# Two bursts of small matmuls joined, the last head's pauses, the prompt state in halves, and longer rows

## The chip, the cores and the metric

The kernel runs on one core of a Trainium2 chip. The metric is the time of one execution on the device in microseconds (us); the time given for a kernel is the median of its runs. Engines: PE does the matmuls (PEld is its weight load), DVE is the vector engine, ACT the scalar engine, POOL the general one, SP issues most of the DMAs.

## The reference

One step of a decoder layer for a prompt of 256 positions and eight samples of 8 positions each, 320 columns in all, at a width of 2048:

```python
u = x @ w_in
q, k, v, o_pre, i_pre, f_pre, z, xbc, dt_pre = split_columns(u, SPLIT_SIZES)
h_m, C, n, m = mlstm_mixer(...)      # 4 heads of 256; states C (256 x 256), n, m
h_s, S, sconv = ssd_mixer(...)       # 16 heads of 64, 2 groups
mix = concatenate([h_m, h_s]) @ w_out
x = layer_norm(ALPHA * x + mix, ln1_g, ln1_b)
f, fconv = conv_ffn(x, w_up, f_conv_w, f_conv_b, w_down, fconv0)
x = layer_norm(ALPHA * x + f, ln2_g, ln2_b)
```

For the mLSTM heads, with `w_inter`, `w_end` and `decay` from the gates:

```python
num = einsum('btsh,bshe->bthe', s, v) + w_inter[..., None] * einsum('bthd,bhde->bthe', q, C)
C_new = decay[..., None, None] * C + einsum('bsh,bshd,bshe->bhde', w_end, k, v)
```

The samples start from given states (for the mLSTM 8 x 4 matrices of 256 x 256); the prompt starts from zero, and its final state `p_C`, `p_n` is returned as well. All is in float32.

## The kernel before, in words

**The main stream.** The four projections (in, out, up, down) are a stream of matmuls with 128 x 128 weights. Each weight tile is split into a high part (ACT, line 74) and a remainder (DVE, line 75), the activations too (XH/XL, MH/ML, HH/HL, and DH/DL, which the trace calls `big`), and each product is three matmuls: hi x high, hi x low, lo x high. `run_groups` walks over groups of two units (128 output columns each; four units in the first group of a projection) in slices of four 128-deep steps, so twelve matmuls. Splits are issued four slices ahead of their use. Two PSUM banks of eight are held by a group of two.

**The tasks.** All other work (gates, SSD, mLSTM, norms) is written as generators. After each slice `tasks.pump(1300)` lets those that are due take steps: at most six steps, and none more once 1300 ns of planned PE time are used. A clock `tasks.clk` counts planned nanoseconds: 0.424 a column for a matmul of the main stream, so 1628 for a slice, and 1.69 a column for a plain float32 matmul. `yield 500` makes a task due 500 planned ns later, but it resumes only after a slice; a `yield` without a number means 2500. The order in which the Python code issues instructions is the order on every engine and on each DMA queue: an engine that reaches an instruction which must wait holds back all behind it. A PSUM bank can be given out again once its last reader has been issued; the matmul that takes it then waits until that reader is done.

**mLSTM samples** (`ml_chunks`, from line 1156): for each head h and each half x of the samples, the products of q with four states (8 calls with 32 output rows each, 128 x 32 weights) go to one bank, ACT scales them (L1200), POOL's queue sends the wanted rows to `VT` (`gather`, L813). After `yield 500` the updates follow: 8 matmuls with 32 x 128 weights from `kv` into four banks, then DVE (L1212) makes decay x state + update. After `yield 1500` SP stores the states (L1179) and loads those needed two rounds later (L1172); then `yield 5000`.

**Scores and heads.** `ml_scores` for a head h > 1 waits for flag `("pv", h-2)`, has SP fetch a broadcast row (`Mb` from `d_m`, L1067), yields 4000, and then issues DVE, ACT and PE work on it (L1074, L1076, L1081, L1082). `ml_out(h)` waits for `("acc", h)`, set when the last chunk of head h is done, yields 2500, multiplies the scores with `VT` (128 x 258 matmuls), sets `("pv", h)`, and normalizes the head: statistics on DVE, `rsqrt` in three rounds with a pause after each, then scale and bias by ACT (L1261), a last pause, and transposes (L238, with ACT copying out at L1269). Then `o_task` multiplies by the gate (L1284) and `mix_parts` splits the result (L1314, L1315) and sets `("mix", 3)`. The first group of the out projection calls `ensure(("mix", s))` ahead of each slice s.

**The end.** After the down projection the second norm's mean and scale are formed (L1671 to L1675), transposed on PE, copied by DVE to `nbr` (L1682), and for each of four column blocks c three matmuls with `rows` give the bias `w`; ACT scales (L1699) and copies `w` (L1701), POOL adds (L1702), ACT's queue sends `y_sample` (L1704, L1709); for the prompt DVE does it in one operation (L1707) and SP sends it. In between stands `p_state`: the prompt's mLSTM state, for each head two units (e = 0, 1) of matmuls over 258 columns into one bank, a copy by ACT (L1607), a DMA by SP (L1608) and a copy of one column to `pn` by POOL (L193). `pn` is transposed on PE in block 2, copied by ACT (L1692) and sent by POOL (L1693).

**The rows.** `big` tiles (DH, DL, dd) have 16 rows of NX = 322 columns: the first part of the up projection runs on 322 columns, as two more carry the first norm's gain and bias; parts 2 and 3 use 320 of them. XH, MH and HH have rows of 320.

Of the kernel before, what the change touches and what calls it, by code (L numbers as in the profile page):

```python
# [7 lines left out]
F32R = mybir.dt.float32r  # L8
# [5 lines left out]
NT = 320  # L14
# [156 lines left out]
def _hybrid_step(ctx, tc, I, O):  # L171
# [638 lines left out]
    def gather(out, y):  # L810

        for c in range(4):
            gdma(out[8 * c:8 * c + 8], y[32 * c:32 * c + 8])  # L813
# [342 lines left out]
    def ml_chunks():  # L1156

        yield from wait("setup")
        c_src, c_dst = I["state_mlstm_C"][0], O["s_C"][0]
        wb = box["wb"]  # L1160
        n0v = n0f.rearrange("p (b h e) -> p b h e", h=4, e=2)
        cts = {}

        def dram(t, n):
            h, x = divmod(n, 4)
            return [t[2 * x + b, h].rearrange("(e p) f -> p e f", p=128) for b in range(2)]

        def load(n):
            h, x = divmod(n, 4)
            t = mt("T4", [128, 2, 2, 258])  # L1170
            for b, d in enumerate(dram(c_src, n)):
                dma(t[:, b, :, 0:256], d)  # L1172
            pcopy(t[:, :, :, 256:257], n0v[:, 2 * x:2 * x + 2, h, :].unsqueeze(3))
            cts[n] = t

        def store(n):
            t = cts.pop(n)
            for b, d in enumerate(dram(c_dst, n)):
                dma(d, t[:, b, :, 0:256])  # L1179

        for n in range(4):
            load(n)
        yield 2000
        for h in range(4):
            yield from wait(("q", 2 * h + 1))
            qz = box["qz"][h % 2]
            pcopy(qz[:, :, :, 0:8], box["Q"][:, 2 * h:2 * h + 2, 256:NT].rearrange("p e (b t) -> p e b t", t=8))
            flags.add(("qz", h))
            yield from wait(("kv", h))
            kv = box.pop(("kv", h))  # L1190
            yield 5000
            for x in range(2):
                n0 = 4 * h + 2 * x
                ps = bank()
                for e in range(2):
                    for b in range(4):
                        mm(ps[32 * b:32 * b + 32, 0:257], qz[:, e, 4 * x + b, :], cts[n0 + b // 2][:, b % 2, e, 0:257],
                           e == 0, e == 1)
                yi = mt("T2", [128, 258])
                A.activation(yi[:, 0:257], ps[:, 0:257], AF.Copy, scale=TT3[:, x, 96 + h:97 + h])  # L1200
                gather(box["VT"][32 * x:32 * x + 32, 2, h, 0:257], yi[:, 0:257])
                yield 500
                pss = [bank() for _ in range(4)]
                for e in range(2):
                    for b in range(4):
                        r = slice(32 * b, 32 * b + 32)
                        mm(pss[b][:, 256 * e:256 * e + 256], kv[r, 0, x, 128 * e:128 * e + 128], kv[r, 1, x, :], True, True)
                tasks.clk -= 6 * 108
                for b in range(4):
                    bb = 4 * x + b  # L1210
                    cb = cts[n0 + b // 2][:, b % 2, :, 0:256]
                    V.scalar_tensor_tensor(cb, cb, wb[:, h, 64 + bb:65 + bb], pss[b].rearrange("p (e f) -> p e f", e=2),  # L1212
                                           ALU.mult, ALU.add)
                yield 1500
                for n in (n0, n0 + 1):
                    store(n)
                for n in (n0 + 4, n0 + 5):
                    if n < 16:
                        load(n)
                yield 5000 if n0 < 14 else 0  # L1220
            flags.add(("acc", h))

    def ml_out(h):
        if h:
            yield from wait(("pv", h - 1))
        yield from wait(("P", h), *[("v", 2 * h + e) for e in range(2)])
        yield 3000
        VT, P, Q = box["VT"], box.pop(("P", h)), box["Q"]
        num = mt("T4", [128, 3, 258])
        ps = bank()  # L1230
        mm(ps[:, 0:258], P[:, 0:128], VT[:, 0, h, :], True, True)
        A.activation(num[:, 0, :], ps[:, 0:258], AF.Copy)
        yield 0
        ps = bank()
        mm(ps[:, 0:258], P[:, 128:256], VT[:, 0, h, :], True, False)
        mm(ps[:, 0:258], P[:, 256:384], VT[:, 1, h, :], False, True)
        A.activation(num[:, 1, :], ps[:, 0:258], AF.Copy)
        yield 0
        yield from wait(("acc", h))
        yield  # L1240
        ps = bank()
        mm(ps[:, 0:258], P[:, 384:512], VT[:, 2, h, :], True, True)
        A.activation(num[:, 2, :], ps[:, 0:258], AF.Copy)
        flags.add(("pv", h))
        yield
        st6, mv = sm([128, 3, 6]), sm([128, 3, 2])
        for i in range(3):
            V.bn_stats(st6[:, i, :], num[:, i, 0:256])
            V.bn_aggr(mv[:, i, :], st6[:, i, :])
        den, sc, nbias, var = (sm([128, 3]) for _ in range(4))  # L1250
        V.scalar_tensor_tensor(den, num[:, :, 256], -1.0, num[:, :, 256], ALU.mult, ALU.max)
        V.tensor_tensor(den, den, TT1[:, :, 64 + h], ALU.max)
        V.reciprocal(den, den)
        V.tensor_tensor(var, den, den, ALU.mult)
        V.tensor_tensor(var, var, mv[:, :, 1], ALU.mult)
        rs = yield from rsqrt(mp, var, GN_EPS, [128, 3], 1500 if h < 3 else 0)
        V.tensor_tensor(sc, den, rs, ALU.mult)
        V.scalar_tensor_tensor(nbias, mv[:, :, 0], -1.0, sc, ALU.mult, ALU.mult)
        yield
        for i in range(3):  # L1260
            A.activation(num[:, i, 0:256], num[:, i, 0:256], AF.Identity, scale=sc[:, i:i + 1],  # L1261
                         bias=nbias[:, i:i + 1])
        yield from wait(("qz", h))
        yield 8000 if h < 3 else 3000
        for e in range(2):
            ps = bank()
            for i in (2, 0, 1):
                transpose(ps[:, TS[i]], num[:, i, 128 * e:128 * e + 128])
            A.activation(Q[:, 2 * h + e, :], ps[:, 0:NT], AF.Copy, scale=col(C_NM + 2 * h + e))  # L1269
            yield 0  # L1270
        flags.add(("hn", h))
# [73 lines left out]


    fp = ctx.enter_context(tc.tile_pool(name="fp", bufs=1))
    NX = NT + 2
    fr = tile_of(fp, {"big": (3, 16 * NX), "c": (12, 346), "rx": (2, 4 * NT), "rows": (2, 2304), "dg": (2, 384)})

    def fsm(shape, dt=F32):
        return fp.tile(shape, dt, name=nm("fsm"))
# [33 lines left out]
        rx[c] = t  # L1386

    load_rx(0)
    dd = fr("big", [128, 16, NX])
    DH, DL = fr("big", [128, 16, NX], F32R), fr("big", [128, 16, NX], F32R)  # L1390
    s1, s2, kbc = fr("c", [128, NT]), fr("c", [128, NT]), fr("c", [128, NT])

    def out_task(m, ps):
# [191 lines left out]
    def p_operands():  # L1585

        yield from wait(("h", 42), "gb")
        yield 10000
        fin["k"], fin["v"] = [], {}
        for i in range(2):  # L1590
            t = fr("rx", [128, 4, 256])
            dma(t, d_kt[:, i, :, :])
            fin["k"].append(t)
            yield 5000
        for h in range(4):
            for i in range(2):
                fin["v"][i, h] = fr("c", [128, 258])
                dma(fin["v"][i, h], d_vt[:, i, h, :])
            yield 5000

    def p_state(h):
        for e in range(2):
            ps = bank()
            for i in range(2):
                mm(ps[:, 0:258], fin["k"][i][:, h, 128 * e:128 * e + 128], fin["v"][i, h], i == 0, i == 1)
            t = fr("c", [128, 258])
            A.activation(t, ps[:, 0:258], AF.Copy)  # L1607
            dma(O["p_C"][0, 0, h, 128 * e:128 * e + 128, :], t[:, 0:256])  # L1608
            pcopy(pn[:, 2 * h + e:2 * h + e + 1], t[:, 256:257])

    def gb_rows():

# [60 lines left out]
    V.scalar_tensor_tensor(nb2, mv[:, :, 0], -1.0, rs, ALU.mult, ALU.mult)  # L1673
    V.tensor_copy(nbc[:, :, 0:2], bcl(nb2, 2))
    V.tensor_tensor(nbc[:, :, 2], nb2, f32(nbc[:, :, 0]), ALU.subtract)  # L1675
    for h in range(3):
        p_state(h)
    ps = bank()
    for i in range(3):
        transpose(ps[0:5, 128 * i:128 * i + 128], f32(nbc[:, i, :]))  # L1680
    times_g(15, fin["pt"])
    V.tensor_copy(nbr, ps[0:5, 0:384])  # L1682
    ys = O["y_sample"].rearrange("b t f -> (b t) f")
    for c in range(4):
        s = slice(512 * c, 512 * c + 512)
        if c == 1:
            p_state(3)
        if c == 2:
            pt = bank()
            transpose(pt[0:8, 0:128], pn)  # L1690
            po = fsm([8, 128])
            A.activation(po, pt[0:8, 0:128], AF.Copy)  # L1692
            gdma(O["p_n"][0, 0].rearrange("h (e p) -> (h e) p", p=128), po)  # L1693
# [80 lines left out]
```

## Time and profile before

| | us |
|---|---|
| median of 3 runs | 1540.66 (1540.61, 1540.66, 1542.48) |
| the profiled execution: its own time | 1537.98 |
| its span | 1536.2 |
| PE busy in it | 1515.6 (99%) |
| DVE / ACT / POOL busy | 979.2 / 773.3 / 313.5 |

A timeline row has start, duration, engine, line, operation, tiles and shapes, a count where like ones are merged, and in brackets the idle time of the engine before it and what ended it. A matmul's duration there contains its latency: the distance of two starts is what a matmul takes from the stream. A row of groups ends with busy time, mean ns of one, and idle time before. A row of the chain has start, duration and what was at work.

### The profile page before, as it was taken

To read this page: it belongs to the slowest core of one execution; us is meant where nothing else is said; L and a number is where in the kernel's file an instruction comes from. 1 tells how busy PE (TensorE), PEld (TensorE's weight loads), DVE (VectorE), ACT (ScalarE), POOL (GpSimd) and SP (SyncE) were. 2 spreads that over 40 slices of the span, in tenths; PEclk is the share of its full clock that TensorE was granted. 3 is DMA by queue.
4 is the path that set the end of the run, shared out by engine and by line. 5 is a ranking of instruction groups with operands and counts; after the bars stand their busy time and mean duration, and the time that the engine had idled before them with its cause. 6 is when DMAs were issued, how large, how long until landed. Compare 5 with 4: busy or idle time off the path is not lost.

```text
span 1536.2 us, 28188 instructions
## 1 busy us (share of the span) xinstructions
PE 1515.6 (99%) x10534; PEld 1483.4 (97%) x10534; DVE 979.2 (64%) x1946; ACT 773.3 (50%) x1539; POOL 313.5 (20%) x661
## 2 busy tenths in 40 slices
PE   9999999999998999999999999999999999999997
PEld 8999999998988999999999999999999999999996
DVE  5766557566877676777776446556544555656765
ACT  4655434444545454666665345555433555555333
POOL 5313331145411232333230000000000000003202
PEclk9999999999999999999999999999999999999998
DMA  9546677578864664455544454555445555555652
GB/s 266 180 135 178 180 206 225 150 201 264 260 203 157 193 193 131 133 154 151 149 138 148 154 162 142 150 151 152 139 149 155 155 147 149 158 149 165 195 166 96
DMA packets 273221, 258.60 MB, mean 168 GB/s; under 512 B 18866, under 2 KB 267458, under 8 KB 272957
## 3 DMA queue, kind: packets, MB, share of 16 engines
q1 hardware_dynamic: 267484, 252.18, 55.0%
q0 software_dynamic: 4848, 3.91, 1.0%
q8 instruction: 82, 1.34, 0.4%
q10 hardware_dynamic: 752, 0.72, 0.2%
q14 instruction: 55, 0.44, 0.1%
HBM read 233.67 MB, written 22.53 MB: 167 GB/s over the span
## 4 chain that ended last, share of the span: by engine, by line
PE 94%; DVE 2%; DMA 1%; ACT 1%; issue 1%; SPq 0%; POOL 0%; ACTq 0%; POOLq 0%; DVEq 0%
PE bk L232 92%; PE bk L238 2%; DMA T<-d_m 1%; DVE lo L75 0%; DMA T<-x_sample 0%; DMA raw<-w_in 0%; ACT hi L74 0%; POOL big L1702 0%; DVE T L1212 0%; ACT XH L418 0%; SPq L1172 0%; DVE XL L420 0%; DVE HL L1525 0%; DVE rx L1627 0%; ACT T L1261 0%
## 5 line engine op out<-in xcount | busy, mean ns | idle before, releaser
L75 DVE TENSOR_TENSOR lo<-raw,hi 128x512 fp32r<-128x512 f32 (+2 forms) x800 | 555.5, 706 | 380.6 <-ACT hi L74 376.9
L74 ACT ACTIVATE hi<-raw 128x512 fp32r<-128x512 f32 (+2 forms) x800 | 485.6, 616 | 449.4 <-PE bk L232 423.1
L232 PE MATMUL bk<-big,hi 128*128 128x320 f32 (+1 forms) x2752 | 609.4, 310 | 0.0
L232 PEld LDWEIGHTS bk<-big,hi 128*128 128x128 f32 x2752 | 462.1, 188 | 0.0
L232 PE MATMUL bk<-big,lo 128*128 128x320 f32 (+1 forms) x1376 | 426.6, 310 | 0.4 <-DVE lo L75 0.4
L232 PE MATMUL bk<-XH,hi 128*128 128x320 f32 x832 | 265.8, 319 | 0.1
L232 PEld LDWEIGHTS bk<-big,lo 128*128 128x128 f32 x1376 | 259.2, 188 | 0.7 <-DVE lo L75 0.7
L232 PE MATMUL bk<-XL,hi 128*128 128x320 f32 x832 | 258.1, 310 | 0.8 <-DVE XL L420 0.7
L232 PE MATMUL bk<-XH,lo 128*128 128x320 f32 x832 | 257.9, 310 | 0.3 <-DVE lo L75 0.2
L232 PE MATMUL bk<-HH,hi 128*128 128x320 f32 x688 | 214.2, 311 | 0.0
L232 PE MATMUL bk<-HH,lo 128*128 128x320 f32 x688 | 212.6, 309 | 0.0
L232 PE MATMUL bk<-HL,hi 128*128 128x320 f32 x688 | 212.6, 309 | 0.0
L232 PEld LDWEIGHTS bk<-XH,hi 128*128 128x128 f32 x832 | 156.7, 188 | 9.9 <-issue 4.7
L232 PEld LDWEIGHTS bk<-XL,hi 128*128 128x128 f32 x832 | 156.8, 188 | 1.9 <-DVE XL L420 1.3
L232 PEld LDWEIGHTS bk<-XH,lo 128*128 128x128 f32 x832 | 156.7, 188 | 0.8 <-DVE lo L75 0.8
L193 POOL TENSOR_SCALAR fst<-c 128x18 f32<-128x18 f32 x86 | 22.0, 262 | 567.0 <-ACT c L1502 566.9
L1509 DVE SCALAR_TENSOR_TENSOR c<-c,fcol,c 128x336 f32<-128x336 f32 x172 | 97.3, 567 | 58.3 <-ACT c L1507 55.3
L232 PEld LDWEIGHTS bk<-HL,hi 128*128 128x128 f32 x688 | 129.2, 188 | 0.0
L232 PEld LDWEIGHTS bk<-HH,hi 128*128 128x128 f32 x688 | 129.2, 188 | 0.0
L232 PEld LDWEIGHTS bk<-HH,lo 128*128 128x128 f32 x688 | 129.1, 188 | 0.0
L232 PE MATMUL bk<-MH,lo 128*128 128x320 f32 x256 | 79.4, 310 | 2.2 <-DVE lo L75 2.2
L232 PE MATMUL bk<-MH,hi 128*128 128x320 f32 x256 | 79.5, 311 | 0.0
(327 smaller groups left out, 1473.5 us busy)
## 6 DMA issues: line engine op xcount, KB each, us to landing
raw<-ffn_w_up SPq DMA_DIRECT2D x172, 512.0 KB, 3.9
raw<-w_in SPq DMA_DIRECT2D x100, 512.0 KB, 4.0
raw<-ffn_w_down SPq DMA_DIRECT2D x71, 512.0 KB, 3.5
raw<-w_out SPq DMA_DIRECT2D x32, 512.0 KB, 4.2
T<-state_mlstm_C SPq DMA_DIRECT2D x32, 256.0 KB, 4.4
s_C<-T SPq DMA_DIRECT2D x32, 256.0 KB, 4.2
T<-state_ssm SPq DMA_DIRECT2D x8, 512.0 KB, 7.4
s_ssm<-T SPq DMA_DIRECT2D x8, 512.0 KB, 6.1
```

Of the source, the lines that this page charges most:

```text
L74: nc.scalar.activation(h, src, AF.Copy)
L75: nc.vector.tensor_tensor(l, src, h.bitcast(F32), ALU.subtract)
L193: G.tensor_scalar(out, in_, 1.0, 0.0, ALU.mult, ALU.add)
L232: nc.tensor.matmul(out, lhsT=lhsT, rhs=rhs, start=start, stop=stop)
L238: nc.tensor.transpose(out, in_, ident[b:b + p, b:b + p])
L1509: V.scalar_tensor_tensor(c[:, 0:336], xp[:, j:j + 336], fcol[:, j, i:i + 1], c[:, 0:336], ALU.mult, ALU.add)
```

## The change

1. In `ml_chunks` the update matmuls follow the products of q at once; the `yield 500` between them is gone, and the scaling by ACT and the `gather` come behind the update matmuls.
2. For the last head the pauses within `rsqrt` are 700 instead of 0, and the pause ahead of its transposes is 6000 instead of 3000.
3. `p_state` is called with a number of units (halves of a head) instead of a head: three ahead of the transposes of `nbc` (there were six), one behind them, then 2, 1 and 1 ahead of blocks 1, 2 and 3 (there were 2 ahead of block 1). The eight copies to `pn` by POOL, and all that follows from `pn`, stand in block 3 instead of the copies with their units and the rest in block 2.
4. Rows of the `big` tiles are 336 columns apart (1344 bytes) instead of 322 (1288 bytes); as many columns as before are used.

```diff
                         mm(ps[32 * b:32 * b + 32, 0:257], qz[:, e, 4 * x + b, :], cts[n0 + b // 2][:, b % 2, e, 0:257],
                            e == 0, e == 1)
-                yi = mt("T2", [128, 258])
-                A.activation(yi[:, 0:257], ps[:, 0:257], AF.Copy, scale=TT3[:, x, 96 + h:97 + h])
-                gather(box["VT"][32 * x:32 * x + 32, 2, h, 0:257], yi[:, 0:257])
-                yield 500
                 pss = [bank() for _ in range(4)]
...
                 tasks.clk -= 6 * 108
+                yi = mt("T2", [128, 258])
+                A.activation(yi[:, 0:257], ps[:, 0:257], AF.Copy, scale=TT3[:, x, 96 + h:97 + h])
+                gather(box["VT"][32 * x:32 * x + 32, 2, h, 0:257], yi[:, 0:257])
...
-        rs = yield from rsqrt(mp, var, GN_EPS, [128, 3], 1500 if h < 3 else 0)
+        rs = yield from rsqrt(mp, var, GN_EPS, [128, 3], 1500 if h < 3 else 700)
...
-        yield 8000 if h < 3 else 3000
+        yield 8000 if h < 3 else 6000
...
-    NX = NT + 2
-    fr = tile_of(fp, {"big": (3, 16 * NX), "c": (12, 346), ...
+    NX, NP = NT + 2, NT + 16
+    fr = tile_of(fp, {"big": (3, 16 * NP), "c": (12, 346), ...
...
-    dd = fr("big", [128, 16, NX])
-    DH, DL = fr("big", [128, 16, NX], F32R), fr("big", [128, 16, NX], F32R)
+    dd = fr("big", [128, 16, NP])
+    DH, DL = fr("big", [128, 16, NP], F32R), fr("big", [128, 16, NP], F32R)
...
-    def p_state(h):
-        for e in range(2):
+    def p_state(n):
+        for u in range(n):
+            h, e = divmod(len(fin["p"]), 2)
...
-            pcopy(pn[:, 2 * h + e:2 * h + e + 1], t[:, 256:257])
+            fin["p"].append(t)
...
-    for h in range(3):
-        p_state(h)
+    p_state(3)
     ps = bank()
     for i in range(3):
         transpose(ps[0:5, 128 * i:128 * i + 128], f32(nbc[:, i, :]))
+    p_state(1)
     times_g(15, fin["pt"])
...
-        if c == 1:
-            p_state(3)
-        if c == 2:
+        if c:
+            p_state(2 if c == 1 else 1)
+        if c == 3:
+            for i, t in enumerate(fin["p"]):
+                pcopy(pn[:, i:i + 1], t[:, 256:257])
             pt = bank()
             transpose(pt[0:8, 0:128], pn)
```

More of the change, by code (lines that the diff above doesn't have):

```diff
@@ L1347, in _hybrid_step @@
     fp = ctx.enter_context(tc.tile_pool(name="fp", bufs=1))
-    NX = NT + 2
-    fr = tile_of(fp, {"big": (3, 16 * NX), "c": (12, 346), "rx": (2, 4 * NT), "rows": (2, 2304), "dg": (2, 384)})
+    NX, NP = NT + 2, NT + 16
+    fr = tile_of(fp, {"big": (3, 16 * NP), "c": (12, 346), "rx": (2, 4 * NT), "rows": (2, 2304), "dg": (2, 384)})
     def fsm(shape, dt=F32):
@@ L1588, in p_operands @@
         yield 10000
-        fin["k"], fin["v"] = [], {}
+        fin["k"], fin["v"], fin["p"] = [], {}, []
         for i in range(2):
```

## The prediction

> **What bounds the kernel now.** First the page: engines, then the chain that ended last.
>
> ```profile
> PE 1515.6 (99%) x10534; PEld 1483.4 (97%) x10534; DVE 979.2 (64%) x1946; ACT 773.3 (50%) x1539; POOL 313.5 (20%) x661
> PE 94%; DVE 2%; DMA 1%; ACT 1%; issue 1%; SPq 0%; POOL 0%; ACTq 0%; POOLq 0%; DVEq 0%
> ```
>
> PE is the bound over the whole span. A change can gain only where PE stands still, where PE loses time between matmuls without standing still, and in the tail behind its last large matmul. So the second view is PE's waits in the stage that parts 1 and 2 touch, and the third the rows of the timeline in which they stand.
>
> ```profile
> PE bk L238 <- ACT T L1261: 2.4, 1, 2.4
> PE bk L232 <- DVE T L1082: 2.3, 2, 1.5
> PE bk L232 <- DVE lo L75: 1.5, 1, 1.5
> PE bk L232 <- ACT T L1232: 0.5, 1, 0.5
> ```
>
> ```profile
> 379.94 0.47 PE L232 MATMUL bk<-T 32*128 32x256 f32 x5 [1.54 <-DVE T L1082]
> 429.59 0.47 PE L232 MATMUL bk<-T 32*128 32x256 f32 x5 [0.79 <-DVE T L1082]
> 431.17 0.70 PE L232 MATMUL bk<-T,T 128*128 128x258 f32 x2 [0.48 <-ACT T L1232]
> 480.62 0.42 PE L232 MATMUL bk<-MH,lo 128*128 128x320 f32 x1 [1.53 <-DVE lo L75]
> 484.79 0.87 PE L238 MATMUL bk<-ident,T 128*128 128x128 f32 x6 [2.44 <-ACT T L1261]
> ```
>
> The reader is to see that all waits from 300 to 500 us come to 6.7 us and have two places: update matmuls (32x256) that want a bank which the scores (L1082) still hold, and the last head's normalization at 480 to 485 us.
>
> **Part 1, the joined bursts: entries and exits.** A burst also costs its borders:
>
> ```profile
> 445.44 0.31 PE L232 MATMUL bk<-XH,lo 128*128 128x320 f32 x1
> 445.68 1.08 PE L232 MATMUL bk<-T,T 128*32 128x257 f32 x16
> 446.69 0.41 PE L232 MATMUL bk<-XH,hi 128*128 128x320 f32 x1
> 446.94 0.30 PE L232 MATMUL bk<-XL,hi 128*128 128x320 f32 x1
> 460.93 0.31 PE L232 MATMUL bk<-XH,lo 128*128 128x320 f32 x1
> 461.17 0.51 PE L232 MATMUL bk<-T 32*128 32x256 f32 x8
> 461.61 0.41 PE L232 MATMUL bk<-XH,hi 128*128 128x320 f32 x1
> 461.86 0.31 PE L232 MATMUL bk<-XL,hi 128*128 128x320 f32 x1
> 814.94 90.19 PE bk L232 x615
> ```
>
> The last row (of the chain, rows of 320) gives the undisturbed pitch, 90.19 / 615 = 0.147 us. Into either burst the step is 0.24 (445.44 to 445.68, 460.93 to 461.17), so 0.093 is lost; the first main matmul behind it takes 0.25 (446.69 to 446.94), so 0.103. A joined pair saves at most one entry and one exit, 0.196, and eight pairs 1.6 us; at least nothing, if PE pays the same between the two. I take 1.1: between the products (128*32) and the updates (32*128) the tile shape changes too, which may cost one of the two borders.
>
> [...]
>
> **Part 1: the bank waits.** Why were the scores late at 379.94? From the chain and the timeline:
>
> ```profile
> 369.18 6.80 DMA T<-d_m
> 369.99 1.08 PE L232 MATMUL bk<-T,T 128*32 128x257 f32 x16
> 378.97 0.57 DVE T L1081
> ```
>
> The broadcast row was issued at 369.18 and landed at 375.98; DVE stood at the scores until then and let go of their bank at 379.8. The products of q had run at 369.99, ahead of the scores; the updates, one resumption later in the pump, fell behind them. Joined, the updates run with the products and find an older bank: 1.54 goes here, and 0.79 at 429.59 if the same order holds there. I take 2.3; bounds 0 and 2.8 (with the 0.48 behind it). DVE's updates (L1212) then stand ahead of the scores, in time in which DVE waits for the row anyway.
>
> The price: five banks are taken at once, two belong to the main pair, so seven of eight are live. A burst may now wait for a bank just used by other work. Bounds for each of eight: 0 and 1.54, the largest above; nearest is the ACT copy of 0.48, and most banks had a slice (1.76 us) to clear. I take one such wait, 0.5.
>
> **Part 1: sooner chunks, and one new wait.** Without its `yield 500` each of eight rounds needs one slice less; a slice is 12 x 0.147 = 1.76 us, so the last head's accumulator is due about eight slices (14 us) sooner. State loads are issued sooner too, two rounds ahead as now: hidden. But the last `gather` comes behind the update matmuls, and only the store's step (1500) and 2500 lie between it and the last head's product with `VT`: three slices, 5.3 us, where there were four.
>
> ```profile
> L813 POOL DMA_DIRECT2D T<-T x48: 497/503/582, 175.3 to 462.0; - x48
> DMA to landing us min/median/max: 1.6/3.4/5.8
> ```
>
> Four issues of 0.50 and a landing of 3.4 behind the last make some 5, plus ACT's 0.5: about level. Bounds 0 and 2 (a landing of 5.8); I take 0.5 as PE's wait.
>
> **Part 2, the last head's pauses.** DVE around 480 us:
>
> ```profile
> 474.64 0.42 DVE L1248 BATCH_NORM_STATS2 sm<-T 128x6 f32<-128x256 f32 x1
> 479.80 0.16 DVE L1258 SCALAR_TENSOR_TENSOR sm<-sm,sm 128x3 f32<-128x3 f32 x1
> 479.88 1.29 DVE L75 TENSOR_TENSOR lo<-raw,hi 128x512 fp32r<-128x512 f32 x2
> ```
>
> With pauses of 0 statistics, `rsqrt` and scale form one block on DVE from 474.64 to 479.96, 5.3 us, and the remainders `lo` come behind it: PE's 1.53. ACT's scaling is late for the same reason, and the transposes, issued two slices behind it, wait 2.44. With 700 each round of `rsqrt` resumes a slice later, and splits stand between; with 6000 (four slices, 7 us) ACT is done when PE arrives. Gain 3.97, bounds 1 (as much DVE work remains) and 4.0; I take 4.0. The pauses cost three slices more in `rsqrt` and two more ahead of the transposes, five in all, while the head starts about eight sooner: the transposes end up about three slices ahead of 484.79, near the start of the out projection. `("mix", 3)` is needed only at that group's thirteenth slice, so the pauses lengthen nothing. If that lead were gone, the transposes would move to about the tenth slice of the out projection, still two ahead of the need.
>
> **Part 4, the rows.** Pitch of the two kinds of up projection, from the chain, windows without other work:
>
> ```profile
> 659.99 140.14 PE bk L232 x942
> 949.93 150.11 PE bk L232 x1022
> ```
>
> On 322 columns 140.14 / 942 = 148.77 ns, on 320 columns of the same rows 150.11 / 1022 = 146.88, and on rows of 320 (above) 146.65. So rows of 1288 bytes cost 0.23 ns a matmul: 2784 in parts 2 and 3 give 0.64 us. The 1344 matmuls on 322 columns should take 146.65 x 322/320 = 147.57 at best: between 0.23 and 1.20 each, 0.3 to 1.6 us. I take 0.5, near the 320-column difference: 1.1 in all, bounds 0 and 2.2. No other engine's count changes.
>
> **Part 3, the tail.** Five rows of the timeline, and four groups of the view by line over the last 21 us:
>
> ```profile
> 1518.76 0.17 DVE L1675 TENSOR_TENSOR fsm<-fsm,fsm 128x3 fp32r<-128x3 f32 x1
> 1521.37 0.49 PE L238 MATMUL bk<-ident,fsm 128*5 128x128 f32 x3
> 1522.59 0.94 PE L232 MATMUL bk<-rows,dg 5*128 5x512 f32 x3 [0.73 <-DVE dg L1682]
> 1529.31 2.55 POOL L1702 TENSOR_TENSOR big<-big,rows 64x512 f32<-64x512 f32 x2
> 1531.89 0.47 ACTq L1709 DMA_DIRECT2D y_sample<-big  x1
> L1699 ACT ACTIVATE big<-big,fsm 64x512 f32<-64x512 f32 x4 | 2.9, 717 | 0.5 <-DVE big L1707 0.4
> L1701 ACT ACTIVATE rows<-bk 64x512 f32<-64x512 f32 x4 | 2.4, 588 | 0.4 <-PE bk L232 0.4
> L193 POOL TENSOR_SCALAR fsm<-c 128x1 f32<-128x1 f32 x8 | 1.5, 190 | 3.5 <-ACT c L1607 3.3
> L1692 ACT ACTIVATE fsm<-bk 8x128 f32<-8x128 f32 x1 | 0.3, 267 | 0.0
> ```
>
> The operand of the transposes is ready at 518.93 (1518.93 us), but they start at 1521.37, behind six units. With three units ahead they start at 1519.05, so block 0 starts at 1520.3 instead of 1522.59, 2.3 sooner. Blocks 0 to 2 keep that lead: POOL's third add, whose end was 1529.31 + 1.28 = 1530.59, ends near 1528.3. Here the change adds a wait. In block 3 the eight copies stand on POOL behind that add, though their data are old; the transpose of `pn` on PE waits for them, the last three matmuls stand behind it on PE, and ACT's copy L1692 stands ahead of block 3's scaling. In a row: 8 x 0.19 = 1.5 to 1529.8; transpose and first matmul 0.3; L1692 with its handover 0.4; L1699 0.72; L1701 0.59 and handover 0.15: POOL's last add starts near 1532.0 and ends near 1533.3, where `y_sample` left at 1531.89. That is 1.4 later. Bounds: 2.3 later (copies at 0.3 each with issue) and, if none of this were serial, 2.3 sooner. I take +1.4, the sum of the rows.
>
> **The sum.** -1.1 (borders) - 2.3 (bank waits) + 0.5 (new bank wait) + 0.5 (`gather`) - 4.0 (last head) - 1.1 (rows) + 1.4 (tail) = -6.1. The profiled execution took 1537.98, 2.7 below the median; it would take 1531.9, and the median of 1540.66 becomes 1534.6, 0.40% less. What the runs can tell from no change is about 0.2%, 3.1 us.
>
> **The rivals.**
> - The waits reappear elsewhere. The same DVE, ACT and SP work is done, and `d_m` still needs 6.8 us; with each round shorter, splits or banks may be late at other slices. Against: DVE is 64% busy and each wait has one named cause of order. Without the 4.0 and the 2.3 the sum is +0.2: 1540.9.
> - Slower: the joined burst waits for banks. Place: the fourth or fifth bank of each of eight bursts, held by other work's reader on DVE or ACT. Price: 1.54 each, as at 379.94, 12.3 in place of -2.3 + 0.5: the sum becomes +8.0, 1548.7. It turns the sign from 0.54 a burst. For: seven of eight banks live. Against: all eight bursts of q and six of eight update bursts now start without a wait. [...]
> - The tail gains. If POOL's copies or the transpose do not hold block 3, the end comes 2.3 sooner instead of 1.4 later: 1530.9. Against: the order in the code.
>
> **How the numbers follow.** Forecast 0.70 (its own range 1530.5 to 1538.5), waits reappear 0.14, slower by banks 0.08, tail gains 0.08. The range from 1530.5 to 1541 leaves out the slow rival and little else. Faster by over 0.2% is most of the first and the last, 0.74; within 0.2% the rest of the first and most of the second, 0.17; slower 0.09.
>
> **What would show it.** [...] No waits for L75 and L1261 near the start of the out projection; last transposes at or ahead of its start. Pitch 146.65 in parts 2 and 3 of the up projection, below 148.5 in the first. In the tail the transposes of `nbc` start 0.1 us behind L1675 instead of 2.4, and eight copies stand in a row on POOL ahead of the last add. The forecast is wrong if the scores or `gather` stop PE for over 3 us, or the pitch does not fall.

## The result, and the profile after

The changed kernel takes 1528.29 us (median of 4 runs, 1527.44 to 1529.56) where the kernel before took 1541.57 on the same occasion (4 runs, 1540.61 to 1543.21): a ratio of 0.992, with a 95% interval of 0.9907 to 0.9932. Forecast were 1534.6 and a range from 1530.5 to 1541: the sign is right, the gain is more than double, and the time lies below the range. The profiled executions took 1537.98 before and 1527.44 after (span 1525.3), 10.5 less.

The engines, from the page of the changed kernel:

```profile
PE 1511.8 (99%) x10534; PEld 1481.1 (97%) x10534; DVE 983.6 (64%) x1946; ACT 771.9 (51%) x1538; POOL 315.2 (21%) x661
```

As many matmuls as before, on the engine that bounds as before; it is busy 3.8 us less in a span that is 10.8 us shorter. Where they went is read by cutting both traces at the same matmuls of the main stream (its number 1824, 2784 and so on, counted from the start):

| stage | before | after |
|---|---|---|
| start to main matmul 1824 | 335.3 | 334.8 |
| 1824 to 2784: the mLSTM samples, all bursts, the last head | 185.26 | 175.70 |
| to 3264: rest of the out projection | 70.65 | 70.40 |
| up and down projections | 923.69 | 922.74 |
| behind the last main matmul | 21.26 | 21.75 |

So 9.56 of the 10.8 lie in one stage. The view of windows has a row for it (start and end, length, PE's busy time and instructions, granted clock, DMA share, GB/s); of before, then of after:

```profile
335.31:520.57 185.26, 177.80 (x1291) 0.99 0.68 214
```

```profile
334.75:510.45 175.70, 173.81 (x1292) 1.00 0.71 225
```

PE stood for 185.26 - 177.80 = 7.46 us before and for 1.89 after: 5.6 less, which is near what the forecast had for all waits together (-2.3 - 4.0 + 0.5 + 0.5 = -5.3). The other 4.0 are in PE's busy time with as many matmuls, and the clock column shows the first part of them. The windows around the wait of 1.54 us at 379.94 in the kernel before:

```profile
378.00:380.00 2.00, 0.46 (x8) 1.00 0.00 0
380.00:382.00 2.00, 2.00 (x12) 0.75 0.24 31
382.00:384.00 2.00, 2.00 (x10) 0.50 0.96 322
384.00:386.00 2.00, 2.00 (x12) 0.90 1.08 372
368.00:432.00 64.00, 61.19 (x454) 0.97 0.75 235
```

PE stands until 379.94, and from about 381 to 384.4 it is granted half its clock: 10 to 12 matmuls in 2 us instead of 14. In the records of this stage ten main matmuls follow each other at 0.267 us instead of 0.147, 1.2 us, and the four small ones behind them are slower too (from the main matmul ahead of them to the next behind 1.17 us, 383.70 to 384.87, where the changed kernel takes 0.83, 418.56 to 419.39): some 1.5 for the whole interval. The forecast priced this wait at its 1.54 alone. The changed kernel has no such interval in the stage:

```profile
368.00:432.00 64.00, 62.51 (x477) 1.00 0.78 245
```

That leaves 9.56 - 5.57 - 1.5 = 2.5 us for borders and small matmuls. The changed kernel's waits from 300 to 500 us (who waited for whom: us in total, times, the longest), and the bursts in the timeline:

```profile
PE bk L232 <- DVE T L1274: 1.2, 1, 1.2
PE bk L232 <- ACT T L1231: 0.3, 1, 0.3
```

```profile
...
398.52 1.08 PE L232 MATMUL bk<-T,T 128*32 128x257 f32 x16
399.53 0.51 PE L232 MATMUL bk<-T 32*128 32x256 f32 x8
...
413.46 1.07 PE L232 MATMUL bk<-T,T 128*32 128x257 f32 x16
414.47 0.38 PE L232 MATMUL bk<-T 32*128 32x256 f32 x3
416.07 0.50 PE L232 MATMUL bk<-T 32*128 32x256 f32 x5 [1.22 <-DVE T L1274]
416.85 0.41 PE L232 MATMUL bk<-XH,hi 128*128 128x320 f32 x1 [0.28 <-ACT T L1231]
...
469.88 0.82 PE L238 MATMUL bk<-ident,T 128*128 128x128 f32 x6
```

The waits for L1082, L75 and L1261 are gone. One joined burst waits for a bank: its fourth update needs the one that `o_task` reads. On DVE that read stands behind an earlier head's statistics and `rsqrt`, and behind a split:

```profile
414.93 0.68 DVE L75 TENSOR_TENSOR lo<-raw,hi 128x512 fp32r<-128x512 f32 x1
415.54 0.48 DVE L1274 COPY T<-bk 128x320 f32<-128x320 f32 x1
```

The last head's transposes stand at 469.88, 3.5 us behind the out projection's first matmul on the high parts (466.36); before they stood at 484.79, 13.9 behind theirs (470.94). So they are earlier than before, but not ahead of its start. The pitch in the up projection's first part and in its second, from the chain:

```profile
659.94 140.16 PE bk L232 x946
934.89 166.17 PE bk L232 x1133
```

140.16 / 946 = 148.16 ns (148.77 before) and 166.17 / 1133 = 146.66 (146.88). And the tail:

```profile
1507.41 0.17 DVE L1677 TENSOR_TENSOR fsm<-fsm,fsm 128x3 fp32r<-128x3 f32 x1
1507.72 0.49 PE L238 MATMUL bk<-ident,fsm 128*5 128x128 f32 x3
1515.73 1.26 POOL L1706 TENSOR_TENSOR big<-big,rows 64x512 f32<-64x512 f32 x1 [0.70 <-ACT rows L1705]
1517.08 1.24 POOL L193 TENSOR_SCALAR fsm<-c 128x1 f32<-128x1 f32 x8
1518.38 0.27 PE L238 MATMUL bk<-ident,fsm 128*8 128x128 f32 x1 [2.55 <-POOL fsm L193]
1520.45 1.26 POOL L1706 TENSOR_TENSOR big<-big,rows 64x512 f32<-64x512 f32 x1 [0.57 <-issue]
1521.74 0.47 ACTq L1713 DMA_DIRECT2D y_sample<-big  x1
```

The transposes of `nbc` start 0.14 behind their operand, and the eight copies hold PE for 2.55 and with it POOL's last add, as forecast.

### The profile page after: what moved, and what is told of

Read it like the earlier page. It is cut to its first block, busy times and chain, and to the rows that moved or that the text cites. A ratio compares the mean times of both kernels' runs of the same rounds, so it can differ in the third digit from the quotient of the medians.

```text
span 1525.3 us, 28171 instructions
## 1 busy us (share of the span) xinstructions
PE 1511.8 (99%) x10534; PEld 1481.1 (97%) x10534; DVE 983.6 (64%) x1946; ACT 771.9 (51%) x1538; POOL 315.2 (21%) x661
## 4 chain that ended last, share of the span: by engine, by line
PE 96%; DVE 2%; ACT 1%; issue 1%; DMA 0%; POOL 0%; POOLq 0%; ACTq 0%; SPq 0%; DVEq 0%
PE bk L232 93%; PE bk L238 2%; DVE lo L75 1%; ACT hi L74 0%; DMA T<-d_m 0%; DVE HL L1525 0%; DVE XL L420 0%; DVE rx L1629 0%; ACT XH L418 0%; DVE big L1553 0%; POOLq L1774 0%; DVE T L1074 0%; ACT L967 0%; DVE rows L1630 0%; POOL big L1706 0%
## 5 line engine op out<-in xcount | busy, mean ns | idle before, releaser
L75 DVE TENSOR_TENSOR lo<-raw,hi 128x512 fp32r<-128x512 f32 (+2 forms) x800 | 554.8, 705 | 368.1 <-ACT hi L74 365.5
L1509 DVE SCALAR_TENSOR_TENSOR c<-c,fcol,c 128x336 f32<-128x336 f32 x172 | 97.2, 566 | 58.3 <-ACT c L1507 55.3
```

What stands on the lines that cost most here:

```text
L75: nc.vector.tensor_tensor(l, src, h.bitcast(F32), ALU.subtract)
L1509: V.scalar_tensor_tensor(c[:, 0:336], xp[:, j:j + 336], fcol[:, j, i:i + 1], c[:, 0:336], ALU.mult, ALU.add)
```

## The experiments

Medians, range and count of runs, and the ratio to the kernel before on the same occasion:

| kernel | us | ratio, 95% |
|---|---|---|
| the kernel before, again | 1539.02 (1536.06 to 1542.21, 12) | 0.9996 (0.9985 to 1.0008) |
| part 1 alone | 1528.62 (1528.1 to 1530.84, 6) | 0.9934 (0.9918 to 0.995) |
| part 2 alone | 1536.53 (1532.31 to 1540.19, 12) | 0.9978 (0.9965 to 0.9991) |
| parts 1 and 2 | 1528.01 (1526.48 to 1529.63, 6) | 0.9926 (0.991 to 0.9941) |
| part 4 alone | 1538.01 (1533.9 to 1540.8, 11) | 0.9997 (0.9987 to 1.0007) |
| part 3 alone | 1538.79 (1537.31 to 1541.71, 11) | 1.0001 (0.9992 to 1.001) |
| all parts, copies to `pn` early | 1526.57 (1526.14 to 1530.01, 5) | 0.9925 (0.9913 to 0.9938) |
| all parts, again | 1527.56 (1526.71 to 1530.15, 5) | 0.9929 (0.9916 to 0.9941) |
| part 1, its pause kept behind the burst | 1532.33 (1530.51 to 1533.83, 6) | 0.9959 (0.9945 to 0.9973) |
| before, scores later | 1535.31 (1533.12 to 1538.02, 12) | 0.9973 (0.996 to 0.9986) |
| all parts and 14 short waits | 1576.58 (1573.98 to 1579.04, 4) | 1.0247 (1.0228 to 1.0266) |
| all parts and 14 longer waits | 1619.5 (1615.48 to 1620.29, 4) | 1.0521 (1.0502 to 1.054) |

The kernel before itself had medians of 1539.69, 1538.18 and 1539.31 on the three occasions: the first four rows belong to the first, the next four to the second, the last four to the third.

### The kernel before, again

No edit.

> The kernel before itself, for its spread. Theory (clock): its profiled execution took 1537.98, the timed ones 1540.6 to 1543.2, because behind PE's waits the granted clock falls to one half for some us in some executions and not in others (in the profile only at 381 to 384.5 us, 1.7 us lost); so executions of more time show a lower mean granted clock, about 1.5 us for each 0.001 below 0.996. Rival (offset): the difference is the profiled execution's own and the clock stays 0.996 in all.

1539.02, the same kernel within 0.1%. Its trace has the same waits, but the half clock is in other places: 380 to 384 has 1.00, and these stretches have it:

```profile
430.00:432.00 2.00, 1.86 (x5) 0.59 0.19 30
432.00:434.00 2.00, 2.00 (x10) 0.55 0.90 279
486.00:488.00 2.00, 2.00 (x11) 0.50 0.18 48
```

They lie at its waits at 430 and 485. So whether a wait of this size is followed by a slow interval differs between executions, and one profile shows one draw. Over 35 executions of this kernel on the first occasion the time goes with the mean granted clock (mean times): 1540.73 at 0.994 (3 runs), 1540.48 at 0.995 (11), 1539.96 at 0.996 (10), 1538.24 at 0.997 (7), 1536.34 at 0.998 (4); a fit gives 1.14 us for each 0.001, and 0.99 and 1.92 on the other two occasions. A part of that clock says nothing of waits: in every trace half clock also stands in the tail, in the profile before from 1527.9 to the end, 8.3 us and most of what its mean lacks of 1. The forecast's base, a profiled run 2.7 below the median, has with 0.996 the usual clock (mean of the 35: 0.9959) and lies 2.0 below these runs' mean at 0.996: the clock does not explain why it was low.

### Part 1 alone, part 2 alone, and both

```diff
# part 1
...
-                yield 500
                 pss = [bank() for _ in range(4)]
...
# part 2
-        rs = yield from rsqrt(mp, var, GN_EPS, [128, 3], 1500 if h < 3 else 0)
+        rs = yield from rsqrt(mp, var, GN_EPS, [128, 3], 1500 if h < 3 else 700)
...
-        yield 8000 if h < 3 else 3000
+        yield 8000 if h < 3 else 6000
```

> Part 1 alone on the kernel before. Theory (clock): the two bank waits go with the half clock behind the first (1.5 + 1.7 + 1.3), borders give 1.9, one new bank wait costs 1.5, and the last head's waits of 4.0 stay: -4.9, some 1536.5. Rival (idle alone): the waits cost only their idle time and borders 1.1: -1.8 to -2.9, some 1539.

> Part 2 alone on the kernel before. Theory: both waits of the last head (1.53 and 2.44) go even without the lead that part 1 gives, since the transposes move to about the tenth slice of the out projection, ahead of the thirteenth that needs them: -4.0, some 1537.5. Rival (lead needed): the flag of the fourth slice comes late and PE waits there for 3 to 4 us: within 1 us of before.

> Parts 1 and 2 on the kernel before. Theory (clock): -9.1 as in the stage of the two profiles, and up to 2.5 more where the timed runs of the kernel before hold more half clock: 1530 to 1532.5. Rival (idle alone): -4.0 -1.8 -1.1: some 1535, and the rest of the 13 us comes from rows and tail.

Part 1 alone takes 11.1 us from the kernel before of its occasion, nearly the whole gain, where 4.9 were expected; part 2 alone takes 3.2 (4.0 expected), and on top of part 1 it adds 0.6, within the intervals. The traces say why. Part 1's waits from 300 to 500 us:

```profile
PE bk L232 <- DVE T L1274: 1.3, 1, 1.3
PE bk L238 <- ACT T L1260: 0.4, 1, 0.4
PE bk L232 <- ACT T L1231: 0.3, 1, 0.3
PE bk L232 <- DVE lo L75: 0.2, 1, 0.2
```

The 3.97 of the last head are gone without any longer pause but for 0.6: its statistics run near 455 us instead of 474.64, its transposes at 464.01, before the out projection starts. Part 2 alone leaves the bank waits and takes the last head's:

```profile
PE bk L232 <- DVE T L1082: 1.9, 2, 1.2
PE bk L232 <- ACT T L1232: 0.5, 1, 0.5
PE bk L232 <- DVE lo L75: 0.3, 1, 0.3
```

So the two parts take the same 4 us, and either would do. In part 1's trace the wait for L1274 (1.30, at 416.92) is followed by half clock (0.50 from 418 to 420 us, 9 matmuls); in the changed kernel the same wait of 1.22 is not (1.00, 13 matmuls).

### Part 1 with its pause kept behind the burst

To tell the lead of the last head from the joining itself, the updates still follow the products at once, but the pause stays:

```diff
...
+                yield 500
                 yield 1500
                 for n in (n0, n0 + 1):
```

> Part 1 alone, but with the pause of 500 kept behind the joined burst (yield 500 ahead of the yield 1500), so that matmuls are joined and the rounds are not shortened. Theory: the lead is what takes the last head's waits away in part 1 alone; here those of about 1.5 and 2.4 us are back, while the borders and the bank waits of the scores stay gone: 1531 to 1534, between part 1 alone (1528.6) and the kernel before (1539). Rival (joining itself shifts DVE's work): the last head's waits stay away, 1528 to 1530.

1532.33, 7.0 less than the kernel before of its occasion, where part 1 had 11.1 on the first occasion: some 4 of it are lost. The last head's waits are back, and from 368 to 474 us PE stands for 0.34 in all:

```profile
474.73 0.41 PE L232 MATMUL bk<-MH,lo 128*128 128x320 f32 x1 [1.07 <-DVE lo L75]
478.90 0.88 PE L238 MATMUL bk<-ident,T 128*128 128x128 f32 x6 [2.43 <-ACT T L1261]
```

```profile
368.00:474.00 106.00, 105.66 (x799) 1.00 0.73 230
```

So the lead is worth about 4, as forecast for the last head, but part 1 alone brings it too; the joining itself is worth 7, where the forecast had 1.1 + 2.3 - 0.5 = 2.9. Between the profiles its samples and out projection are 5.3 us shorter than before (250.3 instead of 255.6): 1.9 of standing, 1.5 of half clock, and 1.9 of borders and small matmuls.

### The kernel before, scores later

Of those 7, the bank waits can be taken alone, with the bursts apart: the scores wait longer for their row, so that the updates get ahead of them.

```diff
             dma(Mb, d_m[h:h + 1].broadcast_to([128, NT]))
-            yield 4000
+            yield 12000 if h > 1 else 4000
```

> The kernel before with a longer pause (12000 instead of 4000) ahead of the scores of heads 2 and 3, nothing else: their broadcast row has landed when DVE gets there. Theory (clock): both waits for L1082 and the 0.48 behind the second go, 2.8 us, and with them the half clock that follows in some executions, 1 to 2 us on average: 1534.5 to 1536.5, most clocks 0.997 or 0.998. Rival (idle alone): 1536.5, clocks as before. The last head's waits of 4.0 stay in both.

1535.31, 4.0 less than the kernel before, where these waits came to 2.8 us of standing. Its waits:

```profile
PE bk L232 <- DVE lo L75: 2.1, 1, 2.1
PE bk L238 <- ACT T L1261: 1.4, 1, 1.4
PE bk L232 <- DMA T<-T: 0.3, 1, 0.3
```

None for L1082; the last head's stay at 3.5. The interval of the ratio (0.996 to 0.9986) is wide, 2.1 to 6.2 us, so this alone doesn't prove the extra 1.2; it agrees with it.

### Waits put in by hand

In the changed kernel's second part of the up projection, where nothing else waits, PE is made to wait behind POOL at 14 places, for four copies of 128 x 64 or for ten:

```diff
+    tw = fsm([128, 64])
+    pcopy(tw, ident[:, 0:64])
...
         def up_done(i, ps):
+            if j == 1 and i % 2 == 0:
+                pw = bank()
+                mm(pw[:, 0:2], ones, tw[:, 0:2], True, True)
+                for _ in range(4):          # 10 in the longer one
+                    pcopy(tw, ident[:, 0:64])
+                mm(pw[:, 2:4], ones, tw[:, 0:2], True, True)
```

> The changed kernel with 14 waits put into the second part of the up projection, where PE has no other: two small matmuls with four POOL copies between them, some 1.3 us of idle time each, at every second unit (one in some 14 us). Theory (clock): behind some of them the clock falls to one half for about 3.4 us, 1.8 us lost each; with a share of 0.3: 22 us of idle and borders and 8 of clock, some 1558, clock about 0.993. Rival (idle alone): some 1550, clock 0.997 or 0.998.

> As the one before with ten POOL copies, some 2.9 us of idle time each. Theory (clock): a larger share, 0.7: 45 us of idle and borders and 18 of clock, some 1591, clock about 0.985. Rival (idle alone): some 1573, clock 0.997 or 0.998. What the page gives for each place tells the share.

Both lost more than expected by either theory: 49 and 92 us for 14 places, against the changed kernel's 1527.56 of another occasion (46.9 and 92.4 in the up and down projections of the traces). Part of that is the wait itself, which was longer at every second place: POOL's four copies took 1.23 us at one kind and 2.08 at the other, where DVE was at work beside them. That gives two sizes to compare in one trace; a short place, a long place, and the one short place that differed:

```profile
897.62 0.38 PE L232 MATMUL bk<-fsm,ones 128*128 128x2 f32 x2 [1.37 <-POOL fsm L193]
916.37 0.38 PE L232 MATMUL bk<-fsm,ones 128*128 128x2 f32 x2 [2.29 <-POOL fsm L193]
1036.31 0.38 PE L232 MATMUL bk<-fsm,ones 128*128 128x2 f32 x2 [1.44 <-POOL fsm L193]
```

```profile
894.00:904.00 10.00, 8.63 (x61) 1.00 0.36 105
912.00:922.00 10.00, 7.71 (x44) 0.83 0.30 94
1033.00:1043.00 10.00, 8.56 (x49) 0.83 0.35 105
```

Measured as the time that the next 34 main matmuls come late, the short places lose 1.98 to 2.06 us (six of seven, clock 1.00), and the seventh 3.59; the long ones, whose wait is 0.86 longer, lose 4.44 to 4.46, all seven; the 14 come to 47.0, the 46.9 from above. So a slow interval costs 3.59 - 2.06 = 1.53 us, and 4.45 - 2.06 - 0.86 = 1.53 again. Behind the first four long waits it begins 10, 6, 3 and 0 main matmuls later. With ten copies (waits of about 3.4 and 4.3 us) all 14 places have it, and lose 5.5 to 7.8.

So each of these places cost more than the length of its wait (1.98 to 2.06 us with a wait of about 1.4), and a slow interval came on top at one of seven near 1.4 us and at all seven at 2.3. These sizes are no threshold for the whole kernel: the wait of 2.43 in the kernel with the pause kept, and that of 2.44 in the profile before, were followed by a clock of 1.00.

Where a wait lies counts too. In each trace the slow intervals last 3.41 us, or two such steps on end (with the scores later from about 479 to 486 us), and start whole steps apart, wherever the waits are: in the profile before one lasts from 380.99 to 384.41 and the tail's starts at 1527.87, 336 steps of 3.413 behind its start; in the kernel with 14 short waits the eight behind the short and long places start 34.13, 34.13, 34.13, 17.07, 20.48, 34.13 and 34.13 us after one another. Cut at these steps, the wait of 2.44 in the profile before lies across two of them, with 1.68 us of standing in the first (part of the 1.53 ahead of it is in it) and 1.40 in the second; in the repeated kernel before the wait of 2.44 has 2.11 in one step, and half clock behind it:

```profile
479.98:483.39 3.41, 1.73 (x10) 1.00 0.32 91
483.39:486.81 3.42, 2.02 (x15) 1.00 0.18 63
```

```profile
481.58:484.99 3.41, 1.30 (x9) 1.00 0.50 154
484.99:488.40 3.41, 3.07 (x13) 0.50 0.25 69
```

Over the 14 traces, up to the tail, all 23 steps at full clock in which PE stood for 1.96 us or more were followed by half clock, 6 of the 22 with 1.2 to 1.7 (in the profile before the one with 1.54, not those with 1.27, 1.40 and 1.68; in the changed kernel's not the one with 1.22), and none with less.

### The rows alone, and the tail alone

```diff
# part 4
...
-    dd = fr("big", [128, 16, NX])
+    dd = fr("big", [128, 16, NP])
...
# part 3
...
-            pcopy(pn[:, 2 * h + e:2 * h + e + 1], t[:, 256:257])
+            fin["p"].append(t)
...
```

> Part 4 alone on the kernel before: only the row length. By the pitches of the two profiles (148.72 to 148.38, 146.87 to 146.67, 146.88 to 146.67 ns): -0.5, -0.3 and -0.3, so -1.0 us; the profile shows 146.67 in parts 2 and 3 of the up projection. Rival: the pitch is no effect of the rows and stays at 146.87. The spread of the kernel before (8 us) hides 1 us in the times; the pitch decides.

> Part 3 alone on the kernel before. From the last matmul of the down projection to the end: 21.26 us before, 21.75 in the changed kernel; so +0.5 here, with PE waiting 2.5 us for POOL's eight copies ahead of block 3. Rival (tail gains): the 2.3 us that block 0 starts sooner reach the end: 19 us.

In the traces the rows take 0.95 us from the up and down projections (923.69 to 922.75); the tail behind the last main matmul is 22.08 instead of 21.26 and 21.49 in the two traces of before (over all traces 20.8 to 21.7 without part 3, 21.8 to 22.4 with it). Neither can be told from no change in the times.

### The copies early

All parts, but each copy to `pn` stays with its unit, the transpose of `pn` and what follows stand behind the sample rows' part of block 3, and SP sends `p_n`:

```diff
-            fin["p"].append(t)
+            i = len(fin["p"])
+            pcopy(pn[:, i:i + 1], t[:, 256:257])
+            fin["p"].append(t)
...
-        if c == 3:
-            for i, t in enumerate(fin["p"]):
-                pcopy(pn[:, i:i + 1], t[:, 256:257])
...
```

> The changed kernel, but POOL's copies stand with their units again, and the transpose of pn, ACT's copy and the DMA of p_n stand in block 3 behind POOL's last add. If the wait for the copies is what gives the lead back, PE does not wait for POOL, the last add ends some 3 us sooner and the stretch from the last matmul of the down projection to the end is 18.5 to 19.5 us instead of 21.75: some 1526 in all. Rival (something else ends the tail, such as the DMAs): it stays at 21 or more.

> The changed kernel beside the others of this call: 1527 to 1530, clock 0.997 or 0.998, and one bank wait of about 1.2 us at the second half of head 2.

```profile
1518.34 0.38 PE L238 MATMUL bk<-ident,fsm 128*8 128x128 f32 x1 [0.17 <-POOL fsm L193]
1520.26 0.99 SPq L1712 DMA_DIRECT2D y_prompt<-big  x2
1520.74 0.49 ACTq L1713 DMA_DIRECT2D y_sample<-big  x1
```

PE's wait for POOL falls from 2.55 to 0.17, and `y_sample` leaves at 1520.74 instead of 1521.74; the tail shrinks by 0.4 to 0.5 (21.37, against 21.75 and 21.91), not to 18.5 to 19.5: the rival came. The prompt's last transfers are issued from 1520.26 on, that of `y_sample` at 1520.74; which of them ends last no row here shows. The median, 1526.57, is 1.0 below the changed kernel of the same occasion, and the lowest of all, but the ranges overlap: it is not shown to be faster. The changed kernel again took 1527.56, as expected, but without the bank wait of 1.2.

## Why the prediction was right or wrong

Between the profiled executions 10.8 us of span went, where the sum had 6.1. Point by point:

- **Bank waits, -2.3: the step that failed.** The waits went as described, by the order that was described, but "1.54 goes here" priced a wait at its length and put the clock behind it at nothing. Behind it PE ran at half clock, some 1.5 us more in that execution, and the row that shows it (0.97 from 368 to 432) could be read beforehand. The runs put in its place 1.53 us for each such interval. In the timed runs of the first occasion the mean clock is 0.9959, against 0.9977 for part 1; at 1.14 us for 0.001 that is 2.1 us, an estimate, as the fit is loose.
- **Last head, -4.0: right in size, wrong in cause.** The lead of part 1, put at 14 us "sooner" and then not used against these waits, takes nearly all of them alone. Part 2 would take them without part 1. On the whole sum the mistake cost nothing.
- **Borders, -1.1.** What is left of the stage is 2.5. The step from the products' start to the first update is 1.01 (398.52 to 399.53), as long as from the products to the main stream before (445.68 to 446.69): the border within the pair costs as much as the one that it replaces, and the entry and the exit of a second burst, 0.196 a pair, are both saved, 1.6 for eight. The border between products and updates can be read: the last four products start at 399.20 and the first update at 399.53, 0.33 later, where the fours ahead of them take 0.22 to 0.24. So this change of shape took about 0.1 us here. The 1.1 was the author's estimate between 0 and 1.6, as no row of before has this border; the runs put 1.6 in its place. Some 0.5 of the other 0.9 lies in how the rows count a wait: standing counts from the end of the record ahead of it, 0.31 us from that matmul's start, where in the stream the next one starts after 0.147, so each wait holds the stream 0.16 longer than its row says, and there are three fewer (two instead of five from 300 to 500 us). Where the rest is stays open.
- **New bank wait, +0.5.** One of eight bursts waits, as taken, but 1.22 + 0.28; in the repetition about 0.3 at most. The rival that was to decide the other way, 1.54 at each of eight, did not come.
- **`gather`, +0.5.** No wait.
- **Rows, -1.1.** Measured -0.95: 146.66 and 148.16 as "would show it" had them.
- **Tail, +1.4.** Each step is there (block 0 sooner, the copies behind the third add, `pn`, then the last add), but the end is only 0.5 later, 0.6 to 0.8 in the kernel with part 3 alone. The 1.4 was reckoned at `y_sample`'s issue, and that moved by 1.2: 18.15 us behind the last main matmul instead of 16.98. From there to the end it took 3.60 us instead of 4.28; why is not shown, and tails without part 3 range from 20.8 to 21.7 themselves.
- **Chance.** About 0.8 of the 10.8 lie at the start (0.6) and in the rest of the out projection (0.25), which the change hardly touches.

In sum 4.7 more than forecast: clock 1.5, borders and what else is left of that stage 1.4, tail 0.9, the idle time 0.3, chance 0.8, less 0.15 for the rows, with roundings. In the medians the gain was 13.3 on the occasion of the result and 10.6 in the repetition; nearly all of that difference is in the kernel before (1541.57 and 1538.18), and its cause is not shown.

## What to carry to other kernels

On a kernel that PE bounds, look at the granted clock behind each wait, not only at the wait: in these traces standing of 1.2 to 1.7 us within one step of 3.41 us was followed by half clock in 6 of 22 steps, and standing of 1.96 us or more in all 23, and such an interval, where it was measured, took about 1.5 us more from the stream behind it. Ask of two parts of a change whether they remove the same wait, since then their gains don't add; and take the base from several runs, as one profile has only one draw of such intervals.

## What the hardware showed that was not expected

- Half clock behind short waits: those of 1.30 (part 1 alone), 1.44 and 2.29 (14 short waits) and 1.54 us (the profile before) were each followed by it. The slow intervals of one trace start whole steps of 3.41 us apart, at points that shift against the waits from place to place (10, 6, 3 and 0 main matmuls behind the first four waits of 2.3).
- It is not one size that decides: 1.37 to 1.44 once in seven, 2.29 seven times in seven, 2.43 and 2.44 in three traces not and in two others (the kernel before again, the rows alone) yes. How the steps lie accounts for these five: 1.7 us or less of a step where it was not, 2.1 and 2.3 where it was; why 6 of the 22 steps between 1.2 and 1.7 us were followed by half clock and 16 not (how much of a step holds small matmuls and transposes may count) was not tried.
- POOL's copies of 128 x 64 took 0.31 us each where DVE stood, and 0.52 at the other kind of place, where DVE's operations on two and three operands (L1509, L1518, L75, from 913.53 to 915.88) ran beside them:

```profile
896.34 1.23 POOL L193 TENSOR_SCALAR fsm<-ident 128x64 f32<-128x64 f32 x4 [106.17 <-PE bk L232]
914.23 2.08 POOL L193 TENSOR_SCALAR fsm<-ident 128x64 f32<-128x64 f32 x4 [1.18 <-PE bk L232]
```

- With rows of 1344 bytes instead of 1288 a matmul on 320 columns took 0.2 ns less (146.66 instead of 146.88) and one on 322 columns 0.6 less (148.16 instead of 148.77).
